# Keeping four more blocks of U h from the routing phase and ending the gathers six blocks early in a two-layer decoder kernel

## The chip, the cores and the metric

The kernel runs on one core of a Trainium2 chip. The time is that of the device for one execution, in microseconds (us); less is better. TensorE (PE) multiplies, with its weight loads counted apart (PEld); VectorE (DVE) and ScalarE (ACT) work elementwise; GpSimd (POOL) issues the gathers; SyncE (SP), ACT and POOL issue transfers (SPq, ACTq in the rows).

## The reference, cut to what matters

Two layers, 512 tokens, width 1024, float32. Each layer is a mixer (a gated MLP over chunks and an attention) and then the expert layer PEER, which the change concerns:

```python
q = einsum(h, w_q)                     # 8 heads
v1, i1 = top_k(q1 @ k1.T, 16); v2, i2 = top_k(q2 @ k2.T, 16)
sc, pos = top_k(v1[:, None] + v2[None, :], 16)
eidx = (i1 * 128 + i2) at pos; g = softmax(sc)      # 8 * 16 experts of 16384 per token
ue = take(u_tab, eidx); ve = take(v_tab, eidx)
y = sum_k g_k * gelu(ue_k . h) * ve_k
```

## The kernel before, in words

Per layer the kernel runs a mixer and then `peer`, which has a routing phase (`route_phase`) and a dense phase (`dense_phase`). The last 128 of the 512 tokens are done by gathering: for each of 128 choices, GpSimd gathers one row of U per token, DVE sums its product with `h` into `dots` (L890), and after a gelu it gathers one row of V per token and DVE adds it, weighted, to `ys` (L897). That makes 256 gathers per layer, all in the dense phase, with five buffers `rows`.

The other 384 tokens are done densely, over all 16384 experts in 128 blocks of 128. For a block, PE computes U h (24 matmuls 128x128 by 128x384: float32 split into a high and a low part, three products, eight chunks; L313 to L315), ACT takes the gelu, DVE multiplies it with the block's gate matrix, and PE multiplies the result with the block's V (18 matmuls of 512 columns, `mix`, L963) into six accumulators `yp`. The weights of each block arrive by SP's queue in a buffer `raw` and are split into `whi` and `wlo` by ACT (L85) and DVE (L86).

The first `PRE` blocks of U h are computed already in the routing phase (`prefill`, L645): the gelu's result `ga` is stored by ACT's queue into a DRAM tile `sp` (L656), and in the dense phase read back by SP's queue (L932, `gar<-sp`). I call these the kept blocks, and the others, whose U h is computed in the dense phase by `hidden` (L928, gelu L940), the computed or hidden ones. Ten kept blocks are placed beside the scoring of the heads (`WITH`), the rest beside the routing proper: `route` finds each token block's experts on DVE, and `build` makes the gate matrices: DVE makes one-hot rows, PE multiplies them (`pg`, L827, L828), ACT evacuates them to `sg` (L829), and twelve times per layer ACT's queue stores 2 MB of them (`gd<-sg`, L831). The dense phase reads them back as `gt` (L866).

The order is set in two ways. The program hands out its instructions in an order written by hand, and a planner, which simulates the engines with estimated times, puts each engine's instructions into a fixed sequence from that; each engine then runs its sequence in order. In the routing phase, the pieces of `routing` are handed out evenly over the kept blocks that are left:

```python
TOTAL = (4 * 22.0 + 24 * 4.4) / 0.93
while prefilled[0] < PRE:
    for q, _ in enumerate(prefill()):
        want = TOTAL * (prefilled[0] - 1 - first + (q + 1) / 8) / (PRE - first)
```

In the dense phase, each block's product with V counts one slot and each computed block another; the gathers with their sums are handed out by the slots passed. `ORDER` alternates groups of four computed and four kept blocks; four blocks (`AHEAD` − 1) are started before the first product with V, and the last two blocks' products (`TAIL`) are done accumulator by accumulator so that `yp` can be copied to `yn` (L989, L990), transposed and added to `xT` (L998, L999), together with `ys`:

```python
slots = NK + NK - PRE
while prog[1] < total * (prog[0] - SDELAY) / (slots - SDELAY - SEND):
```

With 60 kept blocks there are 15 groups of them and 17 of computed ones, so that at one place two groups of computed blocks follow each other. The next layer's first five loads are issued by POOL, behind the last gather.

Of the kernel before, what the change touches and what calls it, by code (L numbers as in the profile page):

```python
# [25 lines left out]
H = 8  # L26
NK = 128
EPS = 1e-6
PRE = 60
RAW1 = 5  # L30
RAW2 = 3
GAB = 3
# [1 line left out]

WITH = [0, 1, 1, 2, 1, 2, 1, 2]
SDELAY = 4.0
SEND = 0.0
HP = 50
LAG2, LAG3 = 1, 1
RCUT = 2  # L40
# [80 lines left out]
def tile_trunk(ctx, tc, a, dbg=None):  # L121
# [489 lines left out]

    PG, NG = list(range(PRE // 4)), list(range(PRE // 4, NK // 4))
    ORDER = []
    for i in range(NK // 4):
        k = sum(1 for b in ORDER[::4] if b >= PRE)
        g = NG[k] if k < min(len(NG), (i * len(NG)) // (NK // 4) + 1) else PG[i - k]
        ORDER += range(4 * g, 4 * g + 4)

    def peer(l, ws, part):
        gd = dram.tile([NK // 4, P, TD // 32, P], F32, name=f"gd{l}")  # L620
        sp = dram.tile([PRE, P, TD], F32, name=f"sp{l}")
        with ExitStack() as outer:
# [11 lines left out]
    def route_phase(l, ws, st, gd, sp, hs, eid, gs):  # L634
# [10 lines left out]
            def prefill():  # L645

                b = prefilled[0]
                prefilled[0] += 1
                w = ws.get()
                ps = psA.tile([P, T], F32, tag="A", name="pA")  # L650
                for c in range(NC):
                    mm3(ps[:, :TD], w, c, c, c == 0, c == NC - 1, TD)
                    yield
                ga = r1.tile([P, TD], F32, tag="ga", name="ga", bufs=GAB)
                S.activation(ga, ps[:, :TD], AF.Gelu_apprx_tanh)
                nc.scalar.dma_start(sp[b], ga)  # L656
# [49 lines left out]
            with ExitStack() as s2:  # L706
# [136 lines left out]
                spent, first = 0.0, prefilled[0]  # L843
# [3 lines that stand above are left out]
                        while spent < want:  # L847
# [6 lines left out]
    def dense_phase(l, ws, part, st, gd, sp, hs, eid, gs):  # L854
# [57 lines left out]
            def background():  # L912
                yield from chosen()

            total = 256 * 1.2
            slots = NK + NK - PRE
            bg = background()
            prog = [0.0, 0.0]

            def slot(f):  # L920
                prog[0] += f
                while prog[1] < total * (prog[0] - SDELAY) / (slots - SDELAY - SEND):
                    k = next(bg, None)
# [170 lines left out]
```

## Time and profile before

| | |
|---|---|
| time, median of 3 runs | 2959.67 us (2958.19 to 2960.43) |
| the profiled execution | 2958.53 us, span 2956.8 us, mean TensorE clock 0.984 |
| busy: PE, PEld, DVE, ACT, POOL | 2843.8, 2474.5, 2435.1, 1244.0, 694.7 us |
| transfers | 782.62 MB, mean 265 GB/s |
| routing phase, first layer | about 285 to 691 us |
| dense phase, first layer | about 691 to 1478 us |

The span runs from the first to the last instruction. A busy PE is one with a matmul under way; matmuls are pipelined, so that a mean duration is longer than the distance between two of them. The granted clock is 1.00 at 2.4 GHz and 0.50 at 1.2 GHz. An idle time in square brackets stands ahead of the instruction, with what ended it.

### The profile page before, as it was taken

What the parts mean: (1) busy time and instruction counts of PE and PEld (TensorE: products, weight loads), DVE (VectorE), ACT (ScalarE), POOL (GpSimd) and SP (SyncE); (2) the same over time, 40 slices, a digit from 0 to 9 for tenths busy, and PEclk for the clock granted to TensorE, in tenths of its full rate; (3) what the DMA queues carried; (4) which work ended last, traced back from release to release, by engine and by line L of the source; (5) the groups of instructions that cost most, each with busy time, mean ns of one, the idle gap of its engine ahead of it and who ended that gap; (6) DMA issues with size and microseconds to landing.
All of it is one profiled execution on the core that took longest, in us unless ns stands there. A gap on an engine that the chain in (4) does not pass through costs nothing. (4 is left out here: it accounts for less than half of the span.)

```text
span 2956.8 us, 42190 instructions
## 1 busy us (share of the span) xinstructions
PE 2843.8 (96%) x15258; PEld 2474.5 (84%) x15258; DVE 2435.1 (82%) x4528; ACT 1244.0 (42%) x1736; POOL 694.7 (23%) x616
## 2 busy tenths in 40 slices
PE   7988999999999999999999899999899999999998
PEld 5756899988888898888876578999888888888886
DVE  7876999986788888888885659999687888888888
ACT  4464345544333333333345533555433333333332
POOL 1000000003344434444500000000043444444333
PEclk8999999999999999999999999999999999999999
DMA  8832345889999999999874123568899999999995
GB/s 304 277 114 66 105 152 183 249 268 351 359 332 348 338 328 354 332 351 331 283 244 136 43 79 115 167 212 265 266 386 332 353 326 351 337 336 347 334 350 186
DMA packets 317873, 782.62 MB, mean 265 GB/s; under 512 B 24944, under 2 KB 154000, under 8 KB 317664
## 3 DMA queue, kind: packets, MB, share of 16 engines
q1 hardware_dynamic: 125712, 431.02, 41.8%
q0 software_dynamic: 75408, 273.92, 25.0%
q10 hardware_dynamic: 116544, 74.98, 8.4%
q8 instruction: 119, 1.95, 0.3%
q14 instruction: 90, 0.74, 0.1%
HBM read 703.28 MB, written 76.55 MB: 264 GB/s over the span
## 5 line engine op out<-in xcount | busy, mean ns | idle before, releaser
L313 PE MATMUL pA<-hhi,whi 128*128 128x384 f32 x2048 | 692.6, 338 | 3.9 <-ACT gar L940 3.9
L314 PE MATMUL pA<-hlo,whi 128*128 128x384 f32 x2048 | 691.6, 338 | 0.0
L315 PE MATMUL pA<-hhi,wlo 128*128 128x384 f32 x2048 | 691.5, 338 | 0.0
L881 POOL DMA_INDIRECT rows<-in_u,eid x256 | 332.6, 1299 | 1030.1 <-DMA raw<-in_v 551.1
L85 ACT ACTIVATE whi<-raw 128x1024 fp32r<-128x1024 f32 x329 | 346.9, 1057 | 491.1 <-PE pA L314 286.1
L86 DVE TENSOR_TENSOR wlo<-raw,whi 128x1024 fp32r<-128x1024 f32 x329 | 406.1, 1238 | 134.5 <-ACT whi L85 132.3
L963 PE MATMUL yp<-vlo,whi 128*128 128x512 f32 x1536 | 474.3, 390 | 0.0
L963 PE MATMUL yp<-vhi,wlo 128*128 128x512 f32 x1536 | 473.7, 390 | 0.0
L963 PE MATMUL yp<-vhi,whi 128*128 128x512 f32 x1536 | 473.2, 390 | 0.0
L881 POOL DMA_INDIRECT rows<-in_v,eid x256 | 335.0, 1309 | 426.6 <-DVE junk L890 343.4
L313 PEld LDWEIGHTS pA<-hhi,whi 128*128 128x128 f32 x2048 | 386.0, 188 | 12.7 <-ACT gar L940 4.4
L314 PEld LDWEIGHTS pA<-hlo,whi 128*128 128x128 f32 x2048 | 386.0, 188 | 6.4 <-issue 0.4
L315 PEld LDWEIGHTS pA<-hhi,wlo 128*128 128x128 f32 x2048 | 385.8, 188 | 0.1
L952 ACT ACTIVATE whi<-gar 128x384 fp32r<-128x384 f32 x256 | 134.1, 525 | 546.0 <-PE yp L963 407.6
L86 DVE TENSOR_TENSOR vlo<-raw,vhi 128x1024 fp32r<-128x1024 f32 x256 | 312.6, 1223 | 47.5 <-ACT vhi L85 43.9
L963 PEld LDWEIGHTS yp<-vlo,whi 128*128 128x128 f32 x1536 | 288.4, 188 | 62.1
L963 PEld LDWEIGHTS yp<-vhi,wlo 128*128 128x128 f32 x1536 | 288.3, 188 | 61.2
L963 PEld LDWEIGHTS yp<-vhi,whi 128*128 128x128 f32 x1536 | 286.6, 188 | 51.5
L897 DVE SCALAR_TENSOR_TENSOR ys<-rows,wsp,ys 128x1024 f32<-128x1024 f32 x254 | 325.3, 1281 | 1.1 <-DMA rows<-in_v,eid 0.4
L890 DVE SCALAR_TENSOR_TENSOR junk<-rows,hs 128x1024 bf16<-128x1024 f32 x256 | 312.2, 1220 | 3.7 <-DMA rows<-in_u,eid 3.7
L85 ACT ACTIVATE vhi<-raw 128x1024 fp32r<-128x1024 f32 x256 | 271.3, 1061 | 85.4 <-PE yp L963 78.4
L953 DVE TENSOR_TENSOR wlo<-gar,whi 128x384 fp32r<-128x384 f32 x256 | 142.7, 559 | 104.2 <-ACT whi L952 96.0
(246 smaller groups left out, 3593.3 us busy)
## 6 DMA issues: line engine op xcount, KB each, us to landing
raw<-in_ut SPq DMA_DIRECT2D x256, 512.0 KB
raw<-in_v SPq DMA_DIRECT2D x256, 512.0 KB
gd<-sg ACTq DMA_DIRECT2D x24, 2048.0 KB
gt<-gd SPq DMA_DIRECT2D x64, 768.0 KB
raw<-in_ada_w SPq DMA_DIRECT2D x94, 512.0 KB
raw<-in_w_all SPq DMA_DIRECT2D x66, 512.0 KB
sp<-ga ACTq DMA_DIRECT2D x120, 192.0 KB
gar<-sp SPq DMA_DIRECT2D x120, 192.0 KB
```

The source lines that it names most:

```text
L85: i = self.nc.scalar.activation(hi[:, :n], r, AF.Copy)
L86: j = self.nc.vector.tensor_sub(lo[:, :n], r, hi.bitcast(F32)[:, :n])
L313: PE.matmul(ps, w[0][:, sl], hhi[:, m, :n], start=first, stop=False)
L314: PE.matmul(ps, w[0][:, sl], hlo[:, m, :n], start=False, stop=False)
L315: PE.matmul(ps, w[1][:, sl], hhi[:, m, :n], start=False, stop=last)
L881: tails["dma"] = G.indirect_dma_start(out=r, out_offset=None, in_=table, in_offset=bass.IndirectOffsetOnAxis(ap=eid[:, k : k + 1], axis=0) ...
L890: tc.keep_in_program_order(V.scalar_tensor_tensor(junk, r, 1.0, hs, ALU.mult, ALU.mult, accum_out=dots[:, k : k + 1]))
L897: tc.keep_in_program_order(V.scalar_tensor_tensor(ys, r, wsp[:, k : k + 1], ys, ALU.mult, ALU.add))
L952: S.activation(whi, ga, AF.Copy)
L953: V.tensor_sub(wlo, ga, whi.bitcast(F32))
L963: PE.matmul(yp[tb][e], w[wq][:, tt], vt[vq][:, e * T : (e + 1) * T], start=(i == 0 and wq + vq == 0), stop=(i == NK - 1 and wq == 1))
```

## The change

64 blocks of U h are kept from the routing phase instead of 60, in both layers, so that 64 instead of 68 are computed in the dense phase, and computed and kept groups alternate throughout. The slots of the dense phase become 192 instead of 196, and the gathers are paced so that they end six slots before the last one.

```diff
-PRE = 60
+PRE = 64
...
 SDELAY = 4.0
-SEND = 0.0
+SEND = 6.0
```

## Rows read from the trace of the kernel before

**Rows 1.** The page's first part: busy time, share of the span, instructions

```profile
PE 2843.8 (96%) x15258; PEld 2474.5 (84%) x15258; DVE 2435.1 (82%) x4528; ACT 1244.0 (42%) x1736; POOL 694.7 (23%) x616
```

**Rows 2.** Stretches, middle of both dense phases: us; PE, PEld, DVE, ACT, POOL busy; clock, DMA

```profile
700.00:1440.00 740.00, 740.00 (x3588) 653.96 (x3587) 610.28 (x790) 268.01 (x365) 308.38 (x237) 1.00 0.93 341
2160.00:2900.00 740.00, 740.00 (x3588) 653.93 (x3587) 609.57 (x783) 266.74 (x363) 309.51 (x237) 1.00 0.92 340
```

**Rows 3.** The chain in the second dense phase: start us, us, what

```profile
2226.92 4.12 PE yp L963 x18
...
2235.22 20.44 PE yp L963 x90
...
2259.85 4.12 PE yp L963 x18
```

**Rows 4.** Stretches of both routing phases and their ends

```profile
310.00:505.00 195.00, 195.00 (x1174) 185.44 (x1173) 194.09 (x935) 95.35 (x125) 5.17 (x32) 1.00 0.45 145
505.00:664.00 159.00, 152.09 (x1296) 142.67 (x1296) 139.28 (x136) 84.51 (x139) 0.00 (x0) 1.00 0.85 258
664.00:674.00 10.00, 5.01 (x43) 4.52 (x43) 5.48 (x5) 6.60 (x10) 0.00 (x0) 0.80 0.77 237
674.00:691.00 17.00, 17.00 (x92) 17.00 (x92) 3.89 (x8) 3.34 (x6) 1.02 (x1) 0.92 0.99 342
...
1950.00:2122.00 172.00, 168.88 (x1449) 158.46 (x1449) 156.36 (x161) 96.51 (x155) 0.00 (x0) 1.00 0.85 258
2122.00:2130.00 8.00, 2.50 (x17) 2.10 (x17) 4.72 (x4) 6.60 (x10) 0.00 (x0) 0.85 0.65 208
2130.00:2148.00 18.00, 18.00 (x94) 18.00 (x94) 4.00 (x8) 3.34 (x6) 1.00 (x1) 0.88 0.99 331
```

**Rows 5.** Timeline of ACT and its queue, end of the first routing phase

```profile
656.10 5.31 ACTq L656 DMA_DIRECT2D sp<-ga  x1
...
666.96 2.95 ACT L85 ACTIVATE vhi<-raw 128x1024 fp32r<-128x1024 f32 x3 [3.47 <-DMA sp<-ga]
...
672.83 0.38 ACTq L831 DMA_DIRECT2D gd<-sg  x1
```

**Rows 6.** Timeline of PE, end of the first routing phase

```profile
670.45 0.27 PE L827 MATMUL pg<-o,gh 128*128 128x128 f16 x1 [3.21 <-ACT sg L829]
...
673.24 0.69 PE L313 MATMUL pA<-hhi,whi 128*128 128x384 f32 x1 [1.77 <-ACT gar L940]
...
691.66 0.63 PE L963 MATMUL yp<-vhi,whi 128*128 128x512 f32 x2
```

**Rows 7.** Groups of DVE from 505 to 664 us: count, busy us, mean ns, idle

```profile
L86 DVE TENSOR_TENSOR wlo<-raw,whi 128x1024 fp32r<-128x1024 f32 x27 | 33.1, 1225 | 18.7 <-ACT whi L85 18.7
```

**Rows 8.** Stretch at the end of the first dense phase, columns as above

```profile
1448.00:1472.00 24.00, 24.00 (x113) 20.55 (x112) 22.76 (x22) 5.05 (x7) 17.61 (x14) 1.00 0.80 274
```

**Rows 9.** Timeline of the first dense phase's last microseconds, all engines

```profile
1475.97 0.60 ACT L989 ACTIVATE yn<-yp 128x512 f32<-128x512 f32 x1 [2.12 <-PE yp L963]
...
1476.99 1.28 DVE L897 SCALAR_TENSOR_TENSOR ys<-rows,wsp,ys 128x1024 f32<-128x1024 f32 x1
...
1478.33 0.87 PE L998 MATMUL pT<-ident,ys 128*128 128x128 f32 x6 [0.20 <-DVE ys L897]
1478.69 1.41 DVE L999 SCALAR_TENSOR_TENSOR xT<-pT,mod,xT 128x512 f32<-128x512 f32 x2 [0.42 <-PE pT L998]
```

**Rows 10.** Timeline of PE: the second layer's first projection matmul

```profile
1493.56 0.80 PE L361 MATMUL pnat<-whi,hhi 128*128 128x512 f32 x1 [5.88 <-ACT hhi L305]
```

**Rows 11.** Stretch of the tile `rows` alone: us; DVE, POOL busy; clock, DMA

```profile
700.00:1440.00 740.00, 290.89 (x364) 308.38 (x237) 1.00 0.93 341
```

**Rows 12.** Transfers from 700 to 1440 us: 40 slices, and the gathers' queue

```profile
GB/s 408 335 401 317 374 354 295 373 351 301 360 323 352 356 301 393 340 318 357 312 320 331 381 367 290 378 319 324 369 313 380 349 290 384 327 322 354 321 387 201
...
q0 software_dynamic: 34009, 123.81, 44.9%
```

## The prediction

> **What bounds the kernel now.** I read the page's busy times first, then the stretches, the chain, and the timeline of the places where TensorE (PE) rests. PE is busy 2843.8 us of 2956.8, the VectorE (DVE) 2435.1 [rows 1]. In the middle of each dense phase PE is busy 740.00 of 740 us, DVE 610, GpSimd (POOL) 308 [rows 2]: that phase is PE's. Its prices come from the chain: the products with V of five kept blocks take 20.44 us, 4.09 each. A block computed there and then makes the period 8.30 us (2235.22 − 2226.92), so a hidden block costs 4.2 us of PE; 24.63 − 20.44, from the next two rows, gives 4.2 again [rows 3].
>
> The routing phase is where the change works. Up to 505 us PE is busy 195.00 of 195 and DVE 194.09: both are full. From 505 to 664 PE is busy 152.09 of 159 (6.9 us idle) and DVE 139.28; in the other layer PE 168.88 of 172 (3.1 idle). At the phase's end PE works 5.01 of 10 us (5.0 idle), in the other layer 2.50 of 8 (5.5 idle). In the 17 and 18 us behind that the granted clock is 0.92 and 0.88 on average, a mix of 2.4 and 1.2 GHz: 0.08 × 17 = 1.4 us and 0.12 × 18 = 2.2 us lost [rows 4]. The reader is to see how little there is to win: 10.0 us in the builds, 10.5 at the two ends and 3.6 in clock, together 24.1. More PE work in the routing phase can fill no more than that.
>
> Why PE rests there: ScalarE (ACT) issues the store of a kept block right behind the 2 MB store `gd<-sg`, and that issue holds its queue for 5.31 us; then an early copy of the dense phase (`vhi`) waits 3.47 us for the kept block to land [rows 5]. The last evacuations `sg` are queued behind it, so PE waits 3.21 us for `sg`, then 1.77 for the gelu of a hidden block, also on ACT [rows 6]. PE takes its instructions in a fixed order, and it had nothing else ahead of those.
>
> **The change part by part.**
>
> *Four blocks per layer move.* Sixty kept and 68 computed blocks per layer become 64 and 64. The dense phase loses 4 × 4.2 = 16.8 us of PE per layer, and there PE is full, so all of it counts. The routing phase gains 4 × 24 matmuls at the same price, 16.8 us. Where PE is full that cancels exactly; the gain is only what falls into idle time. The weights' splitting moves along: 1.22 us of DVE per block [rows 7], 4.9 per layer. From 505 on DVE has 19.7 us free; ahead of 505 it is full, but PE is too and is lengthened by 4.2 us per block, which hides 1.2 of DVE. The four gelus are ACT's in either phase. On SP's queue four loads of `in_ut` come earlier, and in the dense phase four reads of 192 KB take the place of four of 512 KB. Nothing new waits on that queue. The one place with two groups of computed blocks in a row disappears; PE's work is the same in any order. All this costs nothing beside the cancelling 16.8.
>
> *How much falls into idle time.* The routing work is handed out over 54 prefills instead of 50, so 8% more PE work stands between two pieces of it. 27 of the 50 blocks were split in the builds [rows 7], so some two of the four new ones fall there: 8 us against 6.9 and 3.1 idle. If the idle time is for lack of work, all of it goes, 10.0 us. If it is only ACT's blocked queue, nothing goes: the build's matmul still stands in PE's queue ahead of the prefill and waits for `sg`. No row decides, since the stops end with ACT, but PE reached them after short work; I take half, 5.0. At the phase's end PE had used up the prefills and was at hidden blocks when it stopped [rows 6]. Four more prefills are 16.8 us of work against 5 of stop, but the planner's order knows nothing of the 5.31 us. So again between nothing and all of 10.5 + 3.6; I take half, 7.0.
>
> *Four more stores per layer on ACT's queue.* A store is only held up when it follows a `gd` store, and those stay 12 per layer. If each of the eight new stores met one, at 6.9 us idle over the 12 of the first layer they would cost 0.6 each, 4.8 together; if none does, nothing. I take 1.5, two or three of them.
>
> *Pacing (SEND).* The 256 gathers and their sums on DVE are handed out over 192 − 4 − 6 = 182 slots instead of 196 − 4 = 192: 5.5% faster, and none beside the last six blocks, 25 us. At the end of the dense phase DVE is busy 22.76 of 24 us [rows 8], above the 610 of 740 of the middle: the sums lag there. The last `ys` stands on DVE until after the last copy of `yn`, at 1476.99, and the transposes of `ys` wait for it until 1478.33; the first `xT` follows at 1478.69. With `ys` done long before, the first `xT` needs the copy that ends at 1476.57 and a few transposes of 0.15 us: about 1477.4 [rows 9]. That is 1.2 us per layer; the lower bound is 0.2, the wait of those transposes, if the ones of `yn` still all go first. I take 1.2, 2.4 for both layers. On POOL the next layer's first loads stand behind the last gather and may issue 25 us earlier; that brings nothing, since the next layer's first matmul waited for `hhi`, not for weights [rows 10].
>
> *What the faster pace costs.* The gathers' sums take DVE 290.9 of 740 us [rows 11]; 5.5% more is 16 us, so DVE goes from 610 to 626 and POOL from 308 to 325, both far from 740. The DMA queues move 341 GB/s in that window [rows 2]; the gathers' 123.8 MB of it become 130.6 and the rest grows by 1%: some 352 GB/s. Single stretches already run at 401 and 408 GB/s [rows 12] while PE never rests [rows 2]. I take 0; the price without that cover is the last rival's.
>
> **The sum**, against the profiled execution's own 2958.5 us (span 2956.8 and 1.7 around it; the median of the runs is 1.1 higher): − 5.0 − 7.0 + 1.5 − 2.4 = − 12.9, so 2945.6 there and 2946.7 as a median, rounded 2947.
>
> **The rivals** (times as medians).
>
> *Nothing fills.* ACT's queue, not missing work, makes each stop, and only the ends' 2.4 us remain: 2959.7 − 2.4 = 2957.3. For it: every stop shown ends with ACT. Against: PE went into the last one with its prefills spent.
>
> *All fills.* 24.1 + 2.4 less: 2933.2. It asks that the new blocks stand in PE's queue just where ACT is held up.
>
> *A worse end of routing, slower.* From the last `gd` store at 672.83 [rows 5] to the first `yp` at 691.66 [rows 6] are 18.8 us, which PE fills with the hidden blocks left. If the last kept block, which now comes later against the build, lands so late that a second copy waits for it ahead of the last evacuations, a stop of the kind seen comes twice: 10.5 + 3.6 more, 2957.3 + 14.1 = 2971.4. It decides from the point where the hidden blocks left are worth less than 18.8 us.
>
> *DMA becomes the bound in the dense phase, slower.* If 341 GB/s were all that there is, the phase could shrink only by the bytes saved, four times 320 KB, 1.3 MB, 3.8 us instead of 16.8: 13 us per layer, 2947 + 26 = 2973. Against it stand the 401 and 408 GB/s. The Trainium skill, "DMA: Bandwidth & Descriptors", section "Bandwidth", holds that HBM to SBUF transfers bind at about 358 GB/s a core. As a limit on every stretch it would make PE wait already now, and this trace, with 408, does not agree. As a limit on the mean it would leave my 352 just under it, and the sum would stay.
>
> **How the numbers follow.** Chances: about half fills (2938 to 2953) 0.42, all fills 0.18, nothing fills 0.25, worse end 0.08, DMA 0.07. A change of 0.2%, 5.9 us, is about what a measurement of this kernel tells from none. Faster 0.42 + 0.18 = 0.60, same 0.25, slower 0.15. The range leaves out the last two: low 2931, all filled less the runs' spread of 2.2; high 2967, nothing filled plus one layer's stop repeated (5.5 + 2.2) and the spread.
>
> **What would show it.** Right: 128 gelus of each kind; PE's idle time between 505 us and the first `yp` under half of its 12 us, and less of the lower clock behind it; PE full in a dense phase shorter by 16.8 us; `ys` done ahead of the last `yn`, and no transpose waiting for it. Wrong: idle PE in the builds and at the end as before (nothing fills); a wait of PE for `sg` longer than 3.21 us, or one for `gt` ahead of the first `yp` (worse end); PE waiting for weights, or DVE for `rows`, in the dense phase (DMA).

## The result, and the profile after

The change made the kernel slower. Five runs of the changed kernel have a median of 2976.93 us (2971.34 to 2977.73), five of the kernel before beside them 2959.61 (2956.68 to 2960.43): a ratio of 1.0061, 95% interval 1.005 to 1.0073. The forecast was 2947 (2931 to 2967), with 0.15 on slower. The profiled execution took 2974.16 us, its span is 2972.4, 15.6 longer than before.

Three marks in each layer show where the 15.6 us are: the first `pq` (routing begins), the first `yp` (the first product with V) and the first `xT` (the dense phase is over).

| start, us | first `pq` | first `yp` | first `xT` | routing | dense |
|---|---|---|---|---|---|
| before, layer 0 | 289.2 | 691.7 | 1478.7 | 402.5 | 787.0 |
| after, layer 0 | 292.7 | 701.4 | 1490.4 | 408.7 | 789.0 |
| before, layer 1 | 1749.3 | 2148.5 | 2935.3 | 399.2 | 786.8 |
| after, layer 1 | 1757.4 | 2162.7 | 2950.9 | 405.3 | 788.2 |

The two mixers differ by + 3.5 and − 3.6 us and cancel. The routing phases are 6.2 and 6.1 us longer, and the dense phases, which were to lose the work that the routing phases gained, 2.0 and 1.4 longer. 12.3 + 3.4 − 0.1 is the whole 15.6.

These marks cut the change in two unevenly: of the computed blocks, six stand ahead of the first `yp` before and four after, so that between the marks only two are gone. Counted from the first gather the comparison is plainer. The first gather of a layer is issued at 685.1 and 2141.9 us before, at 700.2 and 2161.5 after: 11.6 and 11.5 us later against the first `pq`. From there to the last product with V PE takes 790.7 us in both layers before and 776.8 after, 13.9 less. From the first to the last gather it is 785.5 us in both layers before, 781.5 and 781.9 after, 4.0 and 3.6 less. So the last gather was issued 5.2 us ahead of the last product before, and 4.7 and 5.1 us behind it after.

The page's busy times, and its chain by engine:

```profile
PE 2847.2 (96%) x15258; PEld 2475.5 (83%) x15258; DVE 2436.4 (82%) x4528; ACT 1243.2 (42%) x1736; POOL 690.2 (23%) x616
...
PE 17%; issue 13%; POOL 8%; DVE 1%; ACTq 1%; ACT 1%; DMA 1%; POOLq 0%; DVEq 0%
POOL rows L881 8%; PE yp L963 4%; PE pA L314 3%; PE pA L313 3%; PE pA L315 3%; ACTq L656 1%; PE pq L314 1%; PE pq L315 1%; PE pg L827 1%; PE pq L313 0%; PE pg L828 0%; ACT sg L829 0%; DMA gd<-sg 0%; PE sc L681 0%; PE ssq L292 0%
```

The instruction counts are those of before, and the busy times within 5 us of them [rows 1]. What is new is POOL at the head of the chain's lines, with the gathers (L881). Before, the same view had no POOL in it:

```profile
PE 38%; DVE 1%; ACT 1%; ACTq 0%; DMA 0%; issue 0%; DVEq 0%
```

Stretches of the changed kernel (us; PE, PEld, DVE, ACT, POOL busy; clock, DMA share, GB/s), from the builds to the end of the first dense phase:

```profile
505.00:664.00 159.00, 154.27 (x1313) 144.80 (x1312) 142.56 (x138) 84.20 (x141) 0.00 (x0) 1.00 0.85 259
664.00:701.00 37.00, 32.79 (x197) 32.09 (x197) 12.80 (x15) 16.52 (x27) 0.75 (x1) 0.91 0.87 291
701.00:1440.00 739.00, 739.00 (x3584) 653.08 (x3583) 604.92 (x785) 265.50 (x362) 303.20 (x235) 1.00 0.93 342
...
1470.00:1480.00 10.00, 7.42 (x33) 5.82 (x31) 7.80 (x7) 0.00 (x0) 8.17 (x7) 0.98 0.82 281
1480.00:1490.00 10.00, 4.89 (x18) 3.39 (x18) 8.86 (x9) 3.07 (x4) 5.20 (x7) 0.51 0.90 320
```

The first two rows answer to the first layer of [rows 4]: PE idles 4.7 and 4.2 us there, before 6.9 and 5.0. The third answers to [rows 2]: PE is full, and POOL and DVE are no busier than before, although the gathers were to go 5.5% faster. The last two are new: PE has run out of work, and from 1480 on the granted clock is half of full speed, 1.2 GHz, after PE had rested from 1477.4 on.

The timeline of the same microseconds, all engines (the answers to [rows 9]):

```profile
1475.69 1.29 DVE L897 SCALAR_TENSOR_TENSOR ys<-rows,wsp,ys 128x1024 f32<-128x1024 f32 x1 [1.00 <-DMA rows<-in_v,eid]
1477.59 1.28 DVE L897 SCALAR_TENSOR_TENSOR ys<-rows,wsp,ys 128x1024 f32<-128x1024 f32 x1 [0.62 <-DMA rows<-in_v,eid]
...
1481.75 1.02 POOL L881 DMA_INDIRECT rows<-in_v,eid  x1 [0.30 <-issue]
1482.04 0.60 ACT L989 ACTIVATE yn<-yp 128x512 f32<-128x512 f32 x1 [15.76 <-DMA rows<-in_v,eid]
1482.69 0.48 PE L998 MATMUL pT<-ident,yn 128*128 128x128 f32 x1 [5.27 <-ACT yn L989]
...
1488.71 1.28 DVE L897 SCALAR_TENSOR_TENSOR ys<-rows,wsp,ys 128x1024 f32<-128x1024 f32 x1 [0.41 <-DMA rows<-in_v,eid]
1490.42 2.07 DVE L999 SCALAR_TENSOR_TENSOR xT<-pT,mod,xT 128x512 f32<-128x512 f32 x3 [0.43 <-PE pT L998]
```

The last product with V is done at 1477.4. The last sum `ys` starts at 1488.71; before it was 1476.99, a moment after the last product [rows 9]. Now sums stand alone behind PE's work, most of them waiting for their row, and the copies `yn` wait too. I call this stretch, in which only gathers and sums are left, the tail. It is what the dense phase lost. Why it is there is the question of the experiments.

One more reading, from the program as built: the place of the sums on DVE among the weights (`wlo`, L953) of the blocks. Ahead of the last block's weights stand 248 of 256 sums in the kernel before, 242 in the changed one; 14 instead of 8 are left for the end.

### The profile page after: what moved, and what is told of

It is laid out like the page before. It is cut to its first block, busy times and chain, and to the rows that moved or that the text cites. A ratio compares the mean times of both kernels' runs of the same rounds, so it can differ in the third digit from the quotient of the medians.

```text
span 2972.4 us, 42231 instructions
## 1 busy us (share of the span) xinstructions
PE 2847.2 (96%) x15258; PEld 2475.5 (83%) x15258; DVE 2436.4 (82%) x4528; ACT 1243.2 (42%) x1736; POOL 690.2 (23%) x616
## 5 line engine op out<-in xcount | busy, mean ns | idle before, releaser
L881 POOL DMA_INDIRECT rows<-in_u,eid x256 | 329.8, 1288 | 1044.4 <-DVE gar L949 576.4
L86 DVE TENSOR_TENSOR wlo<-raw,whi 128x1024 fp32r<-128x1024 f32 x329 | 399.2, 1215 | 160.2 <-ACT whi L85 154.1
L881 POOL DMA_INDIRECT rows<-in_v,eid x256 | 332.2, 1298 | 433.5 <-DVE junk L890 349.8
L953 DVE TENSOR_TENSOR wlo<-gar,whi 128x384 fp32r<-128x384 f32 x256 | 142.1, 555 | 102.5 <-ACT whi L952 98.9
```

The lines of the kernel that those rows point to most:

```text
L86: j = self.nc.vector.tensor_sub(lo[:, :n], r, hi.bitcast(F32)[:, :n])
L881: tails["dma"] = G.indirect_dma_start(out=r, out_offset=None, in_=table, in_offset=bass.IndirectOffsetOnAxis(ap=eid[:, k : k + 1], axis=0) ...
L953: V.tensor_sub(wlo, ga, whi.bitcast(F32))
```

## The experiments

Each was timed in rounds against the kernel before on the same chip. Ratios are to that, with 95% intervals. "Routing" and "dense" are the first layer's, between the marks above.

**One part alone: e1 and e2.**

```diff
 # e1_pre64_send0        # e2_pre60_send6
 PRE = 64                PRE = 60
-SEND = 6.0              SEND = 6.0
+SEND = 0.0
```

> Only the 64 kept blocks; the gathers are handed out as before. Theory A (the chain gather, landing, sum, free buffer has a pace of its own, some 0.32 gathers per us, and the hand-out in the program does not set it): as slow as the changed kernel, 2974 to 2979 us, last layer-0 sum near 1489 us. Theory B (the tighter hand-out does the harm): back to 2945 to 2960 us.

> Only the tighter hand-out of the gathers; 60 kept blocks as before. Theory A: no difference from the kernel before, 2956 to 2963 us, as many gathers by 1400 us (240 give or take 4). Theory B: slower by 10 us or more, 2970 us and up. The forecast's own step (the hand-out moves the sums ahead of the end copies): 2.4 us per layer, 2953 to 2956 us.

e1: 2974.79 us, 1.0061 (1.0044 to 1.0078); routing 409.2, dense 788.9. e2: 2957.45 beside 2957.46, 1.0000 (0.9990 to 1.0009). The 64 blocks do all the harm, the hand-out nothing in either direction. For 64 blocks the program as built is even the same on every engine with SEND 0 and 6. Here the hand-out did not set a sum's place: the planner put it later, as it seems where by its own estimate the row has landed (e10 bears on this). So the step on SEND fell whole: nothing was paced faster, and nothing ended earlier.

**The buffers: e3 and e4.**

```diff
 # e3_rows7
-rows = st.enter_context(tc.tile_pool(name="rows", bufs=5))
+rows = st.enter_context(tc.tile_pool(name="rows", bufs=7))
 # e4_yn_v
-y = rows.tile([P, 1024], F32, tag="rows", name="yn")
+y = vp.tile([P, 1024], F32R, tag=("vhi", "vlo", "vhi")[tb], name="yn").bitcast(F32)
```

> The changed kernel with seven buffers for gathered rows, not five. Theory A (the chain through five buffers sets the end of the dense phase): more gathers stand open at a time, the last sum of layer 0 comes 5 to 15 us sooner, 2950 to 2965 us. Theory C (the transfers themselves are the limit, so that gathers only stand longer in the queue): no gain, 2973 to 2980 us.

> The changed kernel with the three copies of the finished sums yp put in buffers of the v tiles, so that they no longer wait for a buffer of gathered rows. Theory A: the first three transposes of each group come earlier, but the fourth still waits for the last sum ys, so it gains under 4 us in both layers, 2970 to 2977 us. Theory D (the shared buffers are what costs the time): the 11 us that TensorE waits there per layer come back, 2950 to 2960 us.

e3: 2970.52 us, 1.0043 (1.0026 to 1.0059), dense 786.0, between the two expectations; e4: 2975.61, 1.0063 (1.0047 to 1.0080), dense 788.1. Both tails stay. In e4 the copies are early, and nothing else is (timeline of ACT and DVE):

```profile
1474.48 0.60 ACT L989 ACTIVATE yn<-yp 128x512 f32<-128x512 f32 x1 [1.89 <-PE yp L963]
...
1484.84 1.28 DVE L897 SCALAR_TENSOR_TENSOR ys<-rows,wsp,ys 128x1024 f32<-128x1024 f32 x1 [0.46 <-DMA rows<-in_v,eid]
1486.69 5.36 DVE L999 SCALAR_TENSOR_TENSOR xT<-pT,mod,xT 128x512 f32<-128x512 f32 x8 [0.57 <-PE pT L998]
```

So the 15.76 us that ACT waited cost next to nothing by themselves (the dense phase is 0.9 us shorter without them): the transposes need `ys`, and `ys` sets the end. Seven buffers shorten the dense phases by 3.0 and 2.3 us, not by 12: the number of gathers in flight is a small part of it.

**A shorter list of choices, with 64 and 60 blocks: e7 and e8.** The last 16 of 128 choices (32 gathers and sums per layer) are left out in both, so that these kernels do not compute the whole sum over the experts.

```diff
-for j in range(n):
-    if q < NB:
+for j in range(n if q < NB else n - 16):
+    if q < NB - 1 or (q == NB - 1 and j < n - 16):
         u(q * n + j)
```

> The changed kernel without the last 16 of 128 choices (32 of 256 gathers and their sums per layer are left out), so that no gather is left behind the last product. Whatever limits the gathers, the tail is gone: 2940 to 2955 us. With 64 kept blocks worth what the forecast took for the routing phase (10.5 us) it stands 10 us under the next kernel, if nothing falls into idle time it stands level with it.

> The kernel before without the same 16 choices: 60 kept blocks, no tail. 2950 to 2958 us, under the kernel before by the tail that it has, 0 to 4 us per layer. The difference to the one with 64 blocks is what the four blocks alone are worth.

e7: 2951.06 us, 0.9982 (0.9973 to 0.9992); routing 409.5, dense 777.2. e8: 2956.51 beside 2956.88, 1.0001 (0.9991 to 1.0010); dense 785.6. This splits the result in two. Without gathers at the end, four more kept blocks are worth 5.5 us (2956.51 − 2951.06). The kernel before had hardly a tail to lose: leaving out its last 32 gathers gives 0.4 us, and 1.4 and 1.2 us between the marks. And the tail of the changed kernel is worth 789.0 − 777.2 = 11.8 us in the first layer and 788.2 − 777.2 = 11.0 in the second.

**Asking for the gathers sooner: e5, e6, e9.** The multiply ahead of `wlo` is kept in program order, so that the hand-out does set the sums' places.

```diff
 # e5_pin_send6; e6 with SEND = 0.0; e9 with seven buffers rows
-V.tensor_mul(g3, g3, gts[g][:, :, j, :])
+tc.keep_in_program_order(V.tensor_mul(g3, g3, gts[g][:, :, j, :]))
```

> The changed kernel with the multiply of each block's gelu by its weights (gar, line 949) also kept in program order on VectorE, so that the hand-out of the gathers, and with it SEND, now sets their order against the blocks: as built, all 256 sums of a layer stand ahead of the weights of block 124, where the changed kernel has 236 there. Theory A (only the planned order holds the gathers back): TensorE stays full, no tail behind the last product, 2945 to 2957 us, 66 gathers or more per 200 us where the changed kernel has 64. Theory C (the transfers are the limit, and the planned order only follows them): VectorE waits for rows with block weights queued behind it, and TensorE waits in the middle of the dense phase; 2968 to 2985 us.

> The same pinned order with the hand-out of before (SEND 0): 248 sums ahead of block 124, 253 of 256 ahead of the last. Theory A: a tail of three sums, as short as in the kernel before, 2950 to 2960 us. Theory C: 2966 to 2980 us, a little better than the pinned order with SEND 6, since the gathers are asked for more slowly.

> The pinned order with SEND 6 as in e5, with seven buffers for gathered rows, not five. Theory C (the sixteen DMA engines have no more to give): no better than e5, 2995 to 3008 us, again some 345 GB/s in the middle of the dense phase. Theory E (the time from issue to landing of one gather, times five buffers, is the limit): two more in flight bring the pinned order to the end without stops, 2945 to 2965 us.

e5: 3003.17 us, 1.0164 (1.0147 to 1.0181); e6: 2976.29, 1.0070 (1.0053 to 1.0087); e9: 3000.73, 1.0138 (1.0119 to 1.0157). The times are at or above what theory C named, but the stops are of another kind. In e5, from 760 to 1400 us, PE is busy 625.46 of 640, and this is what DVE waited for (us in total, times, longest):

```profile
DVE vlo L86 <- ACT vhi L85: 112.9, 65, 4.3
DVE wlo L86 <- ACT whi L85: 7.0, 4, 2.9
```

No wait for `rows` is among them. With the multiply pinned, DVE stands at a split `vlo`, which waits for ACT's `vhi`, and that for products that PE has still to do (253.7 us in all in this stretch); the next block's weights stand behind it. These three show that this order is bad, not what bounds the gathers; I take them as inconclusive.

**Fewer bytes: e10.** 31 of the 32 loads of `gt` per layer are left out, so all blocks are multiplied with the first group's gate matrix.

```diff
-if g not in gts:
-    load_g(g)
-V.tensor_mul(g3, g3, gts[g][:, :, j, :])
+V.tensor_mul(g3, g3, gts[ORDER[0] // 4][:, :, j, :])
```

> The changed kernel, not pinned, with five buffers, in which 31 of the 32 loads of gt per layer are left out (all blocks take the weights of the first group): 24 MB of 273 less to move in each dense phase, nothing else changed. Theory C: the gathers take the room, 66 or more per 200 us, the tail behind the last product goes, 2940 to 2955 us like the kernel with 16 choices left out. Theory E: gathers as before, 64 per 200 us, 2968 to 2978 us.

e10: 2952.83 us, 0.9978 (0.9967 to 0.9989); dense 777.2, to the tenth that of e7. As built, 131 sums stand ahead of the 64th block's weights where the changed kernel has 115, and all 256 ahead of the 126th's. The gathers took the room that the loads left: stretch from 760 to 1400 us of e10, and of the changed kernel behind it, POOL's count being that of the gathers:

```profile
760.00:1400.00 640.00, 640.00 (x3104) 565.80 (x3103) 544.06 (x699) 231.64 (x314) 301.21 (x220) 1.00 0.91 326
```

```profile
760.00:1400.00 640.00, 640.00 (x3103) 565.64 (x3102) 527.21 (x679) 230.21 (x314) 264.93 (x204) 1.00 0.93 343
```

220 against 204 with the same five buffers. So the way through the buffers (theory E) does not hold the gathers at 204. Whether the chip's transfers do is not shown by this, since the planner made DVE's order anew for e10. In the changed kernel's stretch GpSimd waited for DVE's sums to free a buffer, 361.4 us in all, and for no transfer; DVE waited for one once, 1.7 us, and not for rows; PE never waited. So there the gathers followed DVE's sums, in their order as built.

**e10's order with all bytes: e16.** Is it the chip that can't move the bytes, or the planner that thinks so? DVE's sums, weights and splits are chained in the order in which they stand in e10, but where the program's own order is the other way round the chain leaves the link out; all loads are kept. As built, 125 sums stand ahead of the 64th block's weights, between the changed kernel's 115 and e10's 131, and all 256 ahead of the 126th's.

```diff
+for kind in text:          # e10's order, one letter for each instruction
+    i, at[kind] = at[kind], at[kind] + 1
+    if prev is not None and POS[prev.name] < POS[DVE[kind][i].name]:
+        tc.add_manual_dep(DVE[kind][i], prev.name, ..., reason="order")
+    prev = DVE[kind][i]
```

> The changed kernel with all its loads, and VectorE's sums placed against the blocks' weights as the planner placed them in e10, where 31 of 32 gt loads were left out: 125 sums ahead of the weights of block 64 and all 256 ahead of block 126, where the changed kernel has 115 and 239. Theory C (the transfers are the limit on the chip): the dense phase does not get to e10's 777 us; TensorE stops in its middle, or the tail stays, 785 us and more, 2965 us and up. Theory A (the order alone holds the gathers back, the chip can move 5% more): about 777 to 780 us, 2948 to 2957 us, with 350 GB/s or more from 760 to 1400 us.

e16: 2971.76 us, 1.0044 (1.0029 to 1.0059), dense 786.4: the times that theory C named, with PE stopping in the middle. The stretch, and the waits of DVE for rows and of PE in it:

```profile
760.00:1400.00 640.00, 634.28 (x3057) 558.55 (x3056) 523.84 (x688) 224.67 (x309) 309.85 (x216) 1.00 0.92 349
```

```profile
DVE ys L900 <- DMA rows<-in_v,eid: 4.8, 3, 3.4
DVE junk L893 <- DMA rows<-in_u,eid: 1.7, 3, 0.8
...
PE yp L966 <- DVE vlo L88: 5.7, 4, 3.1
```

The chip moved 349 GB/s instead of 343 and 216 gathers instead of 204 where the order asked for them. The tail is gone: the last sum starts at 1473.1, 17.5 us ahead of the last product at 1490.6. But from the first to the last product it is 785.0 us instead of 775.7, and PE stood for 5.7 of them, so that of the 11.8 us only 2.6 came back.

The times are theory C's; its reason is not shown. DVE waited for rows 6.5 us in this stretch, but 13.9 in e10, where PE was full. Ahead of PE's longest stop (3.1 us, up to 1042.72) DVE had waited for the gelus of two computed blocks, with three splits `vlo` behind them, one of which PE needed. SP, whose loads wait for such splits to free a buffer, issued none from 1020.7 to 1042.75, and the queues ran empty (timeline of DVE, then the stretch):

```profile
1034.27 0.56 DVE L952 TENSOR_TENSOR gar<-gar,gt 128x384 f32<-128x384 f32 x1 [2.90 <-ACT gar L943]
...
1039.83 0.56 DVE L952 TENSOR_TENSOR gar<-gar,gt 128x384 f32<-128x384 f32 x1 [3.80 <-ACT gar L943]
...
1041.44 3.49 DVE L88 TENSOR_TENSOR vlo<-raw,vhi 128x1024 fp32r<-128x1024 f32 x3
```

```profile
1034.00:1043.00 9.00, 5.90 (x32) 5.39 (x31) 4.93 (x7) 0.73 (x2) 2.14 (x2) 1.00 0.31 107
```

So at that stop no load was asked for, and the transfers did not give too little. The changed kernel's order left some room in the transfers unused; how much there is e16 does not tell.

**Moving bytes out of the phase: e11 to e15.** The first gathers of U and their sums go into the builds of the routing phase, one after each quarter of a token block, through one buffer of their own; the queues carry 258 GB/s there [rows 4].

```diff
+def u_early():
+    k = early[0]; early[0] += 1
+    r = cs.tile([P, 1024], F32, tag="rowe", name="rowe")
+    G.indirect_dma_start(out=r, ..., in_=a[f"u{l}"], ...)
+    V.scalar_tensor_tensor(r, r, 1.0, hs, ALU.mult, ALU.mult, accum_out=dots[:, k : k + 1])
...
+u_early()        # ahead of each gd<-sg: 12 (e11); 8, not in the first build (e14);
                  # 16, two at a time, not in the first build (e12)
```

> The changed kernel with 12 of the 256 gathers of each layer, and their sums, moved ahead into the builds of the routing phase, where the queues carry 252 to 280 GB/s; one more buffer there. 4 sums are left behind the last block as built, not 14. Theory C: the tail goes as with 16 choices left out, less what 12 sums of 1.2 us cost where VectorE has some 20 us free: 2948 to 2958 us. Rival: VectorE or the landing of rows stops the builds, and 10 us per layer are lost there: 2968 us and up.

> The changed kernel with 8 gathers and sums moved, one for each quarter of the second and third build. 9 sums are left behind the last block as built (14 in the changed kernel, 8 in the kernel before, 4 in e11). Theory C: a tail as short as before's, most of the gain: 2944 to 2955 us. If the gain of e11 has to do with the first build or with something else, 2960 us and up.

> The same with 16 gathers moved, in the second and third build only; no sum is left behind the last block as built. Theory C: 2946 to 2958 us. Rival as for 12: 2968 us and up.

| | time, us | ratio (95%) | routing | dense |
|---|---|---|---|---|
| e11, 12 moved, 64 kept | 2943.31 | 0.9940 (0.9923 to 0.9958) | 410.9 | 771.1 |
| e14, 8 moved, 64 kept | 2948.01 | 0.9968 (0.9954 to 0.9983) | 410.7 | 773.9 |
| e12, 16 moved, 64 kept | 2993.15 | 1.0116 (1.0098 to 1.0134) | 427.0 | 774.6 |
| e13, 12 moved, 60 kept | 2977.35 | 1.0074 (1.0057 to 1.0090) | 412.6 | 786.0 |
| e15, 12 moved, 68 kept | 2982.49 | 1.0083 (1.0066 to 1.0099) | 436.7 | 766.3 |

In e11, e12 and e14 one to two more computed blocks stand ahead of the first `yp` than in the changed kernel, which alone makes their dense phase 4 to 8 us shorter and their routing phase as much longer. e11 and e14 beat both kernels. e11 is 5 us under its expectation; PE idles only 1.3 us of 159 in its builds (4.7 in the changed kernel), which I had not foreseen, and whether that is all of it is not shown. The end of its dense phase is the one that the forecast had described: the sums done at 1465.5 and the copies set the end.

e12's dense phase is as short, and the rival came true in its routing phase. DVE, ahead of the first weights:

```profile
696.33 1.22 DVE L816 SCALAR_TENSOR_TENSOR rowe<-rowe,hs 128x1024 f32<-128x1024 f32 x1 [7.06 <-DMA rowe<-in_u,eid]
...
703.68 1.23 DVE L816 SCALAR_TENSOR_TENSOR rowe<-rowe,hs 128x1024 f32<-128x1024 f32 x1 [6.12 <-DMA rowe<-in_u,eid]
```

Two at a time through one buffer run behind, and the last moved sums stand ahead of the dense phase's first weights. The other two tell whether moving helps any kernel:

```diff
 # e13_early12_60: e11 with     # e15_early12_68: e11 with
 PRE = 60; SEND = 0.0           PRE = 68
```

> The kernel before (60 kept blocks, SEND 0) with 12 gathers and sums per layer moved into the builds. Its dense phase is bound by TensorE, so theory C gives it nothing for the transfers that go: 2952 to 2960 us, level with the kernel before. Theory F (moved gathers help any kernel of this form): as much as from the changed kernel without its tail, 2951, to e11, 2943: 8 us under the kernel before, 2945 to 2951 us.

> 68 kept blocks, 12 gathers moved. TensorE loses another 16.8 us of the dense phase, the transfers only 1.3 MB; 11 sums are left behind the last block as built. Theory C: the tail is back, and there is little idle time left in the routing phase to fill, so no better than e11: 2943 to 2962 us. Were TensorE's idle time in the routing phase still to be filled, 2935 to 2941 us.

In the dense phase e13 is as theory C has it: 786.0 against the kernel before's 787.0, 1.0 us gained where PE is the bound. Its total is 17 us above the expected range, all in routing: 10.1 and 12.7 us more than before. There DVE waited for a moved row with the next one-hot rows of the build queued behind it (first row), and PE idled 8.5 us of 26 at a clock of 0.64 on average (second, from the stretches):

```profile
660.07 1.22 DVE L816 SCALAR_TENSOR_TENSOR rowe<-rowe,hs 128x1024 f32<-128x1024 f32 x1 [4.46 <-DMA rowe<-in_u,eid]
```

```profile
664.00:690.00 26.00, 17.48 (x127) 16.07 (x128) 16.98 (x16) 12.14 (x20) 0.00 (x0) 0.64 0.84 251
```

e15 missed too. Its dense phase is only 4.8 us shorter than e11's, though PE takes 10.8 us less from the first to the last product, and its last sum starts at 1492.1, after the last product: the tail is back, as C says. But its routing phase is 25.8 us longer for four blocks, at most 16.8 us of work, which I had not allowed for.

## Why the prediction was wrong

*What bounds the kernel* was right for PE and stopped there. "That phase is PE's" holds for the middle of the dense phase in both kernels. The gathers were as near to being the bound: the sums ended with PE's work [rows 9], and leaving 32 gathers out gave only 0.4 us (e8), so before the two just balanced.

*Four blocks per layer move* was right as an exchange of PE work, 16.8 us each way, and so was its other line, unused in the sum: four reads of 192 KB for four of 512 KB. PE lost 16.8 us of work there, the queues 1.3 MB. That "all of it counts" in the dense phase was wrong: PE's part became 13.9 us shorter from the first gather on, the gathers' only 4.0.

*How much falls into idle time* was mis-sized. From 505 us to the first `yp` and its counterpart in the second layer, PE idled 11.9 and 8.6 us before and 8.9 and 6.8 after: 4.8 us filled, where I had 5.0 for the builds and 5.2 of idle time at the ends. The lower clock at the ends stayed: 0.12 × 27.6 = 3.3 us before, 0.09 × 37 = 3.3 after. Of the stop's chain everything is still there, the issue on ACT's queue behind the `gd` store too, 7.28 us where it was 5.31 [rows 5]:

```profile
670.77 0.38 ACTq L831 DMA_DIRECT2D gd<-sg  x1
671.25 7.28 ACTq L656 DMA_DIRECT2D sp<-ga  x1
```

*Four more stores* met a held queue once more per layer: 11 and 10 stores of kept blocks were held for more than 2 us, where it had been 10 and 9. What these cost by themselves, against the 1.5 us taken, no run shows. The forecast for these two steps together was − 10.5 us; e7 against e8 gives − 5.5.

*Pacing (SEND)*, − 2.4 us, was wrong in its mechanism: 0.0 in e2. I read the formula as the pace, though the planner makes the order, and only the order as built tells it.

*What the faster pace costs*, taken as 0, is the step that failed. No faster pace came (e2). The gathers went on at 0.32 per us (204 in 640 us, before 203), PE finished earlier, and what was left of them became a tail of 11.8 and 11.0 us. No term of the sum had the time that the gathers themselves take. The cover for the 0 was "single stretches already run at 401 and 408 GB/s" [rows 12]. Those are peaks of a flow whose mean hardly moves. From 1000 to 1400 us of the changed kernel, in 40 slices:

```profile
GB/s 412 334 372 272 351 406 296 354 279 318 413 322 401 238 353 411 324 373 256 310 410 357 352 287 324 407 323 374 249 360 407 301 369 275 330 409 309 386 263 373
DMA packets 39104, 136.60 MB, mean 341 GB/s; under 512 B 4338, under 2 KB 8437, under 8 KB 39077
```

Slices of 410 stand beside slices of 240 to 280. From 760 to 1400 us the mean was 340 GB/s before, 343 after, 346 with seven buffers, 344 and 348 in e5 and e9 with PE at rest for 14.5 and 8.5 us, and 349 in e16, again at PE's cost. The 352 that my sum needed over the whole phase were reached in none.

*The rivals.* The one that came nearest is the last, DMA as the bound: it let the phase shrink by 3.8 us of bytes instead of 16.8, and gave 13 us per layer and 2973. Measured are 11.4 per layer on average and 2976.9, higher mainly because less idle time was filled. It had 0.07, for the sake of those peaks. Its size is borne out, its reason is not shown: PE never waited for weights in the middle, and DVE waited for `rows` only at the end. How near the price came may be luck in part: it was DVE's order as built, and no wait for transfers, that held the gathers there. The Trainium skill's 358 GB/s beside it ("DMA: Bandwidth & Descriptors", section "Bandwidth") is in the same section the share of a core when both cores of an HBM domain stream, and a core alone is given 425 for 16 MB. This kernel runs on one core, and no run shows 358 to bind it: means over 400 us go up to 352 with PE full (e3, 684 to 1084 us) and to 356 with PE at rest for 1.6 us (e16, 2506 to 2906 us). My reply, that peaks of 408 speak against such a limit, holds for a limit on every stretch and says nothing on the mean. The other rivals left out what set the end.

*The sum, put right:* 2959.6 − 5.5 (e7 against e8) + 22.8 (the two tails) = 2976.9. The agreement to the tenth is luck: with the 2.6 us that the kernel before itself loses in e8 between the marks it is 2974.3, against a profiled execution of 2974.2 and a median of 2976.9.

*What stays open.* Why the gathers go at 0.32 per us with all loads in place. That a shorter list (e7), fewer bytes (e10) or gathers moved ahead (e11, e14) removes the tail or most of it is shown; whether the chip's transfers hold the pace, or the order that the planner makes from its estimates of them, is not. For the transfers speaks that the DMA engines were busy 0.92 to 0.95 of the time; against them, that e16 moved 12 gathers more in 640 us, and that slices of 151 to 218 GB/s stand among its 410s, some of them at PE's stops. e3 moved 356 GB/s from 760 to 1000 us with PE full, and 340 from there to 1400. An order with early sums but without stops of PE was not found.

## What to carry to other kernels

Before moving work off the engine that bounds a phase, see how long each other stream of the phase takes from its own start, here the gathers: if that is within some per cent of the engine's time, take some of it out along with the work (e11 against the changed kernel: 33.6 us from 12 gathers and sums per layer moved). A peak rate in the profile is not room for the mean. A mean that stays the same in every variant is not yet a limit either: the variants can share one order, and e16 moved more once the order asked for it. And a pacing number in a program that a planner reorders may move nothing: look at the built order before pricing it.

## What the runs showed of the hardware

- In the kernels with all loads the first dense phase's mean was between 340 and 349 GB/s from 760 to 1400 us, with the 16 DMA engines' mean busy share at 0.92 to 0.95, while single slices of 10 us reached 413. Most of them share nearly one order of DVE, so this is not shown to be the chip's limit.
- A store of 192 KB issued on ACT's queue right behind a 2 MB one held the queue for 5.34 and 7.28 us at the end of the changed kernel's first routing phase; others there took 0.33.
- In the changed kernel's first tail the transposes of `yn`, most of them in the stretch with a clock of 0.51, took 421 ns in the median; those of `ys`, from 1490.0 on, 273.
- The same instructions in the same order (the changed kernel and e1) had their first `pq` at 292.7 and 288.8 us: marks of one execution are good to about 4 us at the kernel's start, lengths of a phase to about 0.5.
